# Trunk layer in fp32 on one core: the gate block z in a two-product form, and weights and read-outs ranked ahead of the scan

## The chip, the cores and the metric

The kernel runs on one core of a Trainium2 chip. The metric is the device time of one execution in microseconds (us). TensorE is called PE here, VectorE DVE, ScalarE ACT, GpSimd POOL and SyncE SP, as in the profile.

## The reference, cut to what matters

One trunk layer for 256 positions of width 2048: a bidirectional SSD mixer, a cross-attention into 256 memory tokens, a ConvGLU channel mixer, and a final norm. The change lies in the mixer's input part:

```python
proj = u @ w_in
z, xbc, dt_raw = jnp.split(proj, [SSD_INNER, SSD_INNER + SSD_CONV_DIM], axis=-1)
xbc = jax.nn.silu(dwconv(xbc, conv_w, conv_b))
xs, Bm, Cm = jnp.split(xbc, [SSD_INNER, SSD_INNER + SSD_GROUPS * SSD_STATE], axis=-1)
...
y = y_f + y_b + xs * d_skip[:, None]
y = rmsnorm(y.reshape(b, s, SSD_INNER) * jax.nn.silu(z), norm_g)
return y.astype(u.dtype) @ w_out
```

The 4096 columns of z and of xs fall into 8 groups of 512 columns; y_f and y_b are a chunked scan over two chunks of 128 positions in either direction.

## The kernel before, in words

**Products.** Every fp32 operand of the large matrix products is split into a high and a low part, both in fp32r, and a product is the sum of high x high, high x low and low x high. Weights come in raw chunks of 1024 elements a partition (512 KB): `load_weights` has SP fetch the chunk into `raw` (5 buffers), ACT cast it to `w_hi` (L106) and DVE subtract to get `w_lo` (L107); `w_hi` and `w_lo` have 4 buffers each. One chunk serves 8 pairs of a contraction tile of 128 rows and an output tile of 128 features.

There are two forms for a pair. `gemm_feat` takes three matmuls of 256 columns (L152 to L154), each with its own load of weights into PE, and leaves the sum in 256 columns of PSUM: 512 output features fill one `psg` tile (2 banks). `gemm_feat_wide` takes two: `w_hi` against the high and low halves of the activations side by side, 512 columns (L169), and `w_lo` against the high half, 256 columns (L171). The two 256-column halves of its result must then be added: `add_halves` copies one out of PSUM on ACT (L177) and adds the other on DVE (L178). Here 256 features fill a `psg` tile. `psg` has two buffers in all (`ps_g`).

**Groups.** The loop over 8 groups runs project(g+1), project_z(g), scan_group(g). `project` makes xs (512 columns) and bc (256 columns), both in the three-product form, and puts them through the convolution (L362 to L373). `project_z` makes the gate `sz`, one buffer: a multiplication by the norm's factor straight from PSUM on DVE (L386) and a SiLU on ACT (L387). `scan_group` transposes xs and B (L405, L413) and copies them out (L406, L407, L414), forms the chunk states (L419, L420) and then, for each of the two chunks: fetches `r`, a 1 MB broadcast of the decays (L424, one buffer, so its fetch waits for L444 of the chunk before), works on it on ACT and DVE (8 times L435 and L436, then the exponential L438), builds `t` (L441, L442, L444), and multiplies (L448, L453). The results are put together on DVE (L456, L459, L460), where L459 reads `er`, a second broadcast fetched by SP (L398, four transfers, one buffer, free after L460 of the scan before). At the end L464 multiplies by `sz`, and L211, L101 and L102 square and split the result into the activations of the next product. That is w_out, whose first half uses `gemm_feat`.

**What sets the order.** The program is written as above, and a scheduler spreads the instructions of each engine into one fixed order each, by their place in the program and a model of the time. Each engine runs its list in order, and waits where an instruction's operands or buffers are not ready. So a group's scan lies between the matmuls of the next group's projections.

Of the kernel before, what the change touches and what calls it, by code (L numbers as in the profile page):

```python
# [1 line left out]

# [7 lines left out]
F32R = mybir.dt.float32r  # L10
AF = mybir.ActivationFunctionType
ALU = mybir.AluOpType
AX = mybir.AxisListType

P = 128
T = 256
# [20 lines left out]
def kernel(  # L37
# [15 lines left out]
    nc = tc.nc  # L53
# [9 lines left out]
    def sb(pool, shape, tag, dtype=F32, **kw):  # L63
        return pool.tile(shape, dtype, tag=tag, name=tag, **kw)
# [40 lines left out]
    def split_plain(hi, lo, src):  # L105
        nc.scalar.copy(out=hi, in_=src)  # L106
        nc.vector.tensor_tensor(out=lo, in0=src, in1=hi.bitcast(F32), op=ALU.subtract)  # L107

    def load_raw(wv, k0, cols):
        width = sum(n for _, n in cols)  # L110
        kc = 1024 // width
        raw = sb(ring_raw, [P, kc, width], "raw")
        at = 0
        for c0, n in cols:
            nc.sync.dma_start(out=raw[:, :, at:at + n], in_=wv[:, k0:k0 + kc, c0:c0 + n])
            at += n
        return raw

    def load_weights(wv, k0, cols, raw=None):
        width = sum(n for _, n in cols)  # L120
        kc = 1024 // width
        if raw is None:
            raw = load_raw(wv, k0, cols)
        hi = sb(ring, [P, kc, width], "w_hi", F32R)
        lo = sb(ring, [P, kc, width], "w_lo", F32R)
        split_plain(hi, lo, raw)
        return hi, lo

    def kview(w):
# [2 lines left out]
    def gemm_feat(units, wv, cols, k_first=0, first_raw=None):  # L132

        width = sum(n for _, n in cols)
        nft = width // P
        kc = 1024 // width
        nk = 4 * len(units)
        ps = psum_g()
        banks = [ps[:, b, :] for b in range((nft + 1) // 2)]
        for k0 in range(0, nk, kc):  # L140
            hi, lo = load_weights(wv, k_first + k0, cols, first_raw if k0 == 0 else None)
            for kk in range(kc):
                kt = k0 + kk
                uh = units[kt // 4][0][:, kt % 4, :]
                ul = units[kt // 4][1][:, kt % 4, :]
                for ft in range(nft):
                    dst = banks[ft // 2][:, (ft % 2) * T:(ft % 2 + 1) * T]
                    wh = hi[:, kk, ft * P:(ft + 1) * P]
                    wl = lo[:, kk, ft * P:(ft + 1) * P]
                    first = kt == 0 and ft % 2 == 0  # L150
                    last = kt == nk - 1 and (ft % 2 == 1 or ft == nft - 1)
                    nc.tensor.matmul(dst, wh, uh, start=first, stop=False, skip_group_check=True)  # L152
                    nc.tensor.matmul(dst, wh, ul, start=False, stop=False, skip_group_check=True)  # L153
                    nc.tensor.matmul(dst, wl, uh, start=False, stop=last, skip_group_check=True)  # L154
        return banks
# [18 lines left out]

    def add_halves(dst, ps):

        nc.scalar.copy(out=dst, in_=ps[:, :, T:])  # L177
        nc.vector.tensor_tensor(out=dst, in0=ps[:, :, :T], in1=dst, op=ALU.add)  # L178

    def gemm_tok(units, wv, c0, k_first=0):  # L180

# [16 lines left out]
    def two(bank):  # L198
        return bank.rearrange("p (j t) -> p j t", t=T)

    def rows2(r):
        return r.unsqueeze(1).broadcast_to([P, 2, T])
# [24 lines left out]
    def inv_rms(pool, acc, dst, n, tags=("rs_v", "rs_s")):  # L227
        ps = psum_m()
        nc.tensor.matmul(ps[:, :T], ones, acc[:, 0, :], start=True, stop=False)
        nc.tensor.matmul(ps[:, :T], ones, acc[:, 1, :], start=False, stop=True)  # L230
        rsqrt_mean(pool, dst, ps[:, :T], n, tags)
# [9 lines left out]
    w_in_v = kview(w_in)  # L241
# [47 lines left out]
    with tc.tile_pool(name="ssd", bufs=1) as ssd:  # L289
# [85 lines left out]
        def project(g):  # L375
            xs = sb(ssd, [P, 4, T], "xs", bufs=2)
            conv_silu(gemm_feat(units_mix, w_in_v, [(INNER + g * 512, 512)]), [g * 4 + j for j in range(4)], xs)
            bc = sb(ssd, [P, 2, T], "bc", bufs=2)
            conv_silu(gemm_feat(units_mix, w_in_v, [(2 * INNER + g * P, P), (2 * INNER + 1024 + g * P, P)]),
                      [32 + g, 40 + g], bc)  # L380
            return xs, bc

        def project_z(g):
            sz = sb(ssd, [P, 4, T], "sz")
            for b, bank in enumerate(gemm_feat(units_mix, w_in_v, [(g * 512, 512)])):
                nc.vector.tensor_tensor(out=sz[:, 2 * b:2 * b + 2, :], in0=two(bank), in1=rows2(r_mix), op=ALU.mult)  # L386
                nc.scalar.activation(out=sz[:, 2 * b:2 * b + 2, :], in_=sz[:, 2 * b:2 * b + 2, :], func=AF.Silu)  # L387
            return sz

        ecum_v = ecum_d.rearrange("(d g j q) l -> g q d j l", d=2, g=GROUPS, q=2)  # L390
# [77 lines left out]
            units_y.append(unit)  # L468

        nxt = project(0)  # L470
        for g in range(GROUPS):
            cur = nxt
            if g + 1 < GROUPS:
                nxt = project(g + 1)
            sz = project_z(g)
            scan_group(g, *cur, sz)
        inv_rms(ssd, acc_y, r_ssd, INNER, ("cb", "b_tok"))


# [295 lines left out]
```

## Time and profile before

| | |
|---|---|
| median of 3 runs | 1865.58 us (1864.4 to 1865.98) |
| profiled execution | 1863.24 us, of which the span of the trace is 1861.5 us |
| PE busy, share of the span | 99% |
| DVE, ACT busy | 68%, 55% |
| DMA engines busy, mean | 62%, 193 GB/s |

Durations below come from the one profiled execution. A busy share is the part of the span in which an engine ran something; a matmul's duration in a row covers its way through the array, so matmuls that follow each other overlap, and the distance between two starts says what one costs.

### The profile page before, as it was taken

The page shows a single profiled execution, that of the slowest core. Times are in us where ns is not written, and L with a number is a line of the kernel's source. Part 1 is how long each engine was busy: PE and PEld are TensorE (multiplying, and loading weights), DVE is VectorE, ACT ScalarE, POOL GpSimd, SP SyncE. Part 2 cuts the span into 40 slices and gives each one's busy share as a digit, 9 for nine tenths or more (in the row PEclk, how much of TensorE's full clock was granted, in tenths as well). Part 3 has the DMA queues.
Part 4 walks back from the last instruction along what each step waited for, and adds up shares of the span by engine and source line. Part 5 has one row for each costly group of instructions (what it writes and reads, how often), then busy time and mean ns, then how long its engine had stood idle before and what let it go on. Part 6 is the DMA issues. An engine that isn't in the chain of part 4 may idle for free.

```text
span 1861.5 us, 29854 instructions
## 1 busy us (share of the span) xinstructions
PE 1842.3 (99%) x11821; PEld 1663.5 (89%) x11821; DVE 1264.2 (68%) x1792; ACT 1018.2 (55%) x1454; POOL 2.3 (0%) x11
## 2 busy tenths in 40 slices
PE   8999999999999999999999999999999999999997
PEld 8999999999999988888888888888888888888886
DVE  6878888988887756655555667666664456666654
ACT  6667667766775645444444455555553345555443
POOL 0000000000000000000000000000000000000000
PEclk9999999999999999999999999999999999999999
DMA  8667666766766765655655556566666666666563
GB/s 289 198 203 214 199 189 201 219 197 201 215 182 205 244 197 182 184 177 170 176 176 181 164 187 206 179 189 188 191 191 192 193 192 188 185 187 187 190 193 114
DMA packets 289708, 358.94 MB, mean 193 GB/s; under 512 B 11616, under 2 KB 210656, under 8 KB 289056
## 3 DMA queue, kind: packets, MB, share of 16 engines
q1 hardware_dynamic: 289488, 356.76, 62.3%
q8 instruction: 92, 1.51, 0.3%
q14 instruction: 48, 0.39, 0.1%
q0 software_dynamic: 80, 0.28, 0.1%
HBM read 352.60 MB, written 4.39 MB: 192 GB/s over the span
## 4 chain that ended last, share of the span: by engine, by line
PE 99%; DMA 0%; DVE 0%; ACT 0%; SPq 0%; issue 0%; DVEq 0%
PE psg L169 30%; PE psg L171 16%; PE psg L154 10%; PE psg L153 10%; PE psg L152 10%; PE psm L194 6%; PE psm L193 6%; PE psm L195 6%; PE psm L453 1%; PE psm L448 1%; PE psm L419 1%; PE psm L589 0%; PE psm L591 0%; PE psm L590 0%; DMA x<-in_x_dram 0%; PE psm L405 0%
## 5 line engine op out<-in xcount | busy, mean ns | idle before, releaser
L107 DVE TENSOR_TENSOR w_lo<-raw,w_hi 128x1024 fp32r<-128x1024 f32 x618 | 753.7, 1223 | 499.3 <-ACT w_hi L106 497.1
L106 ACT CAST w_hi<-raw 128x1024 fp32r<-128x1024 f32 x618 | 645.7, 1049 | 684.0 <-PE psg L169 314.5
L169 PE MATMUL psg<-unit,w_hi 128*128 128x512 f32 x2432 | 853.3, 396 | 0.0
L171 PE MATMUL psg<-unit,w_lo 128*128 128x256 f32 x2432 | 683.4, 281 | 0.0
L169 PEld LDWEIGHTS psg<-unit,w_hi 128*128 128x128 f32 x2432 | 456.3, 188 | 106.0
L171 PEld LDWEIGHTS psg<-unit,w_lo 128*128 128x128 f32 x2432 | 460.7, 189 | 0.2
L154 PE MATMUL psg<-unit,w_lo 128*128 128x256 f32 x1552 | 444.8, 287 | 0.1
L152 PE MATMUL psg<-unit,w_hi 128*128 128x256 f32 x1552 | 442.4, 285 | 0.0
L153 PE MATMUL psg<-unit,w_hi 128*128 128x256 f32 x1552 | 441.6, 285 | 0.0
L154 PEld LDWEIGHTS psg<-unit,w_lo 128*128 128x128 f32 x1552 | 298.6, 192 | 3.4 <-issue 3.1
L152 PEld LDWEIGHTS psg<-unit,w_hi 128*128 128x128 f32 x1552 | 298.7, 193 | 1.7 <-issue 1.7
L153 PEld LDWEIGHTS psg<-unit,w_hi 128*128 128x128 f32 x1552 | 298.7, 193 | 0.3 <-issue 0.2
L195 PE MATMUL psm<-w_hi,unit 128*128 128x512 f32 x480 | 187.0, 390 | 0.0
L194 PE MATMUL psm<-w_lo,unit 128*128 128x512 f32 x480 | 187.0, 390 | 0.0
L193 PE MATMUL psm<-w_hi,unit 128*128 128x512 f32 x480 | 186.9, 389 | 0.0
L193 PEld LDWEIGHTS psm<-w_hi,unit 128*128 128x128 f32 x480 | 90.1, 188 | 18.9
L195 PEld LDWEIGHTS psm<-w_hi,unit 128*128 128x128 f32 x480 | 90.1, 188 | 18.8
L194 PEld LDWEIGHTS psm<-w_lo,unit 128*128 128x128 f32 x480 | 90.1, 188 | 18.4
L435 ACT ACTIVATE r<-r,ncum_tok 128x128 f32<-128x128 f32 x128 | 39.4, 390 | 57.5 <-DMA r<-cum_d 57.5
L436 DVE SCALAR_TENSOR_TENSOR r<-r,ncum_tok 128x128 f32<-128x128 f32 x128 | 37.0, 347 | 16.7 <-ACT r L435 16.7
L441 ACT ACTIVATE t<-cb,dt_tok 128x128 f32<-128x128 f32 x128 | 39.1, 389 | 0.7 <-DVE cb L428 0.2
L442 DVE SCALAR_TENSOR_TENSOR t<-cb,dt_tok,t 128x128 f32<-128x128 f32 x128 | 36.5, 349 | 3.3 <-ACT t L441 3.3
(222 smaller groups left out, 1076.4 us busy)
## 6 DMA issues: line engine op xcount, KB each, us to landing
raw<-in_w_up_dram SPq DMA_DIRECT2D x176, 512.0 KB, 3.7
raw<-in_w_in_dram SPq DMA_DIRECT2D x130, 512.0 KB, 4.6
raw<-in_w_down_dram SPq DMA_DIRECT2D x88, 512.0 KB, 3.8
raw<-in_w_out_dram SPq DMA_DIRECT2D x64, 512.0 KB, 4.2
raw<-in_wkv_dram SPq DMA_DIRECT2D x64, 512.0 KB, 3.8
raw<-in_w_in_dram SPq DMA_DIRECT2D x64, 256.0 KB, 4.4
r<-cum_d SPq DMA_DIRECT2D x16, 1024.0 KB, 6.3
raw<-in_wq_dram SPq DMA_DIRECT2D x32, 512.0 KB, 3.5
```

Source lines behind the costliest of these rows:

```text
L106: nc.scalar.copy(out=hi, in_=src)
L107: nc.vector.tensor_tensor(out=lo, in0=src, in1=hi.bitcast(F32), op=ALU.subtract)
L152: nc.tensor.matmul(dst, wh, uh, start=first, stop=False, skip_group_check=True)
L153: nc.tensor.matmul(dst, wh, ul, start=False, stop=False, skip_group_check=True)
L154: nc.tensor.matmul(dst, wl, uh, start=False, stop=last, skip_group_check=True)
L169: nc.tensor.matmul(ps[:, ft, :], hi[:, kk, fs], unit[2][:, kt % 4].rearrange("p s t -> p (s t)"), start=(kt == 0), stop=False, skip_group_ ...
L171: nc.tensor.matmul(ps[:, ft, :T], lo[:, kk, fs], unit[0][:, kt % 4, :], start=False, stop=(kt == nk - 1), skip_group_check=True)
L193: nc.tensor.matmul(banks[tt], uh, hi[:, kk, :], start=(kt == 0), stop=False)
L194: nc.tensor.matmul(banks[tt], uh, lo[:, kk, :], start=False, stop=False)
L195: nc.tensor.matmul(banks[tt], ul, hi[:, kk, :], start=False, stop=(kt == nk - 1))
L435: nc.scalar.activation(out=t1[:, h, :], in_=t1[:, h, :], func=AF.Identity, bias=ncum_tok[:, c, hf:hf + 1])
L441: nc.scalar.activation(out=t2[:, h, :], in_=cb[:, 1, :], func=AF.Copy, scale=dt_tok[:, c, hb:hb + 1])
```

## The change

z is computed in the two-product form, in two halves of 256 columns, each read out by `add_halves`; L386's multiplication and the SiLU then work in SBUF. While the groups run, a chunk's fetch and split and the read-outs of `add_halves` are ranked as if they stood 500 instructions earlier in the program, so the scheduler puts them ahead of work of the scan with which they compete. Outside the groups nothing is ranked.

```diff
--- before.py
+++ after.py
@@ -1,4 +1,4 @@
-from contextlib import ExitStack
+from contextlib import ExitStack, nullcontext
 
 import concourse.bass as bass
 import concourse.tile as tile
@@ -116,14 +116,21 @@
             at += n
         return raw
 
+    ahead = [0]
+
+    def urgent():
+
+        return tc.high_priority(offset=ahead[0]) if ahead[0] else nullcontext()
+
     def load_weights(wv, k0, cols, raw=None):
         width = sum(n for _, n in cols)
         kc = 1024 // width
-        if raw is None:
-            raw = load_raw(wv, k0, cols)
-        hi = sb(ring, [P, kc, width], "w_hi", F32R)
-        lo = sb(ring, [P, kc, width], "w_lo", F32R)
-        split_plain(hi, lo, raw)
+        with urgent():
+            if raw is None:
+                raw = load_raw(wv, k0, cols)
+            hi = sb(ring, [P, kc, width], "w_hi", F32R)
+            lo = sb(ring, [P, kc, width], "w_lo", F32R)
+            split_plain(hi, lo, raw)
         return hi, lo
 
     def kview(w):
@@ -174,8 +181,9 @@
 
     def add_halves(dst, ps):
 
-        nc.scalar.copy(out=dst, in_=ps[:, :, T:])
-        nc.vector.tensor_tensor(out=dst, in0=ps[:, :, :T], in1=dst, op=ALU.add)
+        with urgent():
+            nc.scalar.copy(out=dst, in_=ps[:, :, T:])
+            nc.vector.tensor_tensor(out=dst, in0=ps[:, :, :T], in1=dst, op=ALU.add)
 
     def gemm_tok(units, wv, c0, k_first=0):
 
@@ -382,9 +390,11 @@
 
         def project_z(g):
             sz = sb(ssd, [P, 4, T], "sz")
-            for b, bank in enumerate(gemm_feat(units_mix, w_in_v, [(g * 512, 512)])):
-                nc.vector.tensor_tensor(out=sz[:, 2 * b:2 * b + 2, :], in0=two(bank), in1=rows2(r_mix), op=ALU.mult)
-                nc.scalar.activation(out=sz[:, 2 * b:2 * b + 2, :], in_=sz[:, 2 * b:2 * b + 2, :], func=AF.Silu)
+            for b in range(2):
+                sv = sz[:, 2 * b:2 * b + 2, :]
+                add_halves(sv, gemm_feat_wide(units_mix, w_in_v, [(g * 512 + b * 256, 256)]))
+                nc.vector.tensor_tensor(out=sv, in0=sv, in1=rows2(r_mix), op=ALU.mult)
+                nc.scalar.activation(out=sv, in_=sv, func=AF.Silu)
             return sz
 
         ecum_v = ecum_d.rearrange("(d g j q) l -> g q d j l", d=2, g=GROUPS, q=2)
@@ -468,12 +478,14 @@
             units_y.append(unit)
 
         nxt = project(0)
+        ahead[0] = 500
         for g in range(GROUPS):
             cur = nxt
             if g + 1 < GROUPS:
                 nxt = project(g + 1)
             sz = project_z(g)
             scan_group(g, *cur, sz)
+        ahead[0] = 0
         inv_rms(ssd, acc_y, r_ssd, INNER, ("cb", "b_tok"))
```

The lines of the gemm functions move by 7 (L152 becomes L159, L169 L176, L177 L185, L178 L186), those of the convolution by 8 and those of the scan by 10 (L435 becomes L445).

The rows that follow are each engine's list: the line, the operation, output and inputs, the output's shape, the engines or DMA queues whose semaphores it waits for (the number 49 is only the program's), and how many like it follow each other.

**PE, last group.** PE's list from the transposes of the last scan (L405) on, before; `psg` is there the first tile of w_out, `psm` tiles belong to the scan:

```order
L405 MATMUL psm<-ident,xs 128x128 [waits PE_49]
L405 MATMUL psm<-ident,xs 128x128 x3
L405 MATMUL psm<-ident,xs 128x128 [waits PE_49]
L405 MATMUL psm<-ident,xs 128x128 x3
L413 MATMUL psm<-ident,bc 128x128 [waits PE_49]
L413 MATMUL psm<-ident,bc 128x128
L154 MATMUL psg<-unit,w_lo 128x256
L152 MATMUL psg<-unit,w_hi 128x256
L153 MATMUL psg<-unit,w_hi 128x256
```

The same place with the change, where L415 is the transpose, L429 the states, L458 the multiplication with them, and L159 to L161 are w_out's first tile:

```order
L415 MATMUL psm<-ident,xs 128x128 [waits PE_49]
L415 MATMUL psm<-ident,xs 128x128 x3
L415 MATMUL psm<-ident,xs 128x128 [waits PE_49]
L415 MATMUL psm<-ident,xs 128x128 x3
L423 MATMUL psm<-ident,bc 128x128 [waits PE_49]
L423 MATMUL psm<-ident,bc 128x128
L429 MATMUL psm<-xsd,b_tok 128x512 [waits DVE_49,Activation_49]
L429 MATMUL psm<-xsd,b_tok 128x512 [waits DVE_49,PE_49]
L436 MATMUL psm<-bc 128x128
L458 MATMUL psm<-bc,st 128x128 [waits Activation_49]
L458 MATMUL psm<-bc,st 128x128 x3
L159 MATMUL psg<-unit,w_hi 128x256 [waits DVE_49]
```

Before, w_out's matmuls of an already opened tile follow the transposes, 29 of them ahead of the first L419, 38 in all ahead of the second; with the change the scan's matmuls stand in a row, and the first matmul of w_out comes behind them and waits for DVE, where the one that releases its buffer is L186 of z's first half.

**ACT, last group.** ACT's list from the work on `r` (L435) on, before; L420 is the states' copy, L438 the exponential, L211 and L101 belong to the end of the scan before the last:

```order
L435 ACTIVATE r<-r,ncum_tok 128x128 [waits DMAHW1_49,DVE_49]
L414 COPY b_tok<-psm 128x256 [waits PE_49]
L435 ACTIVATE r<-r,ncum_tok 128x128 x7
L106 CAST w_hi<-raw 128x1024 [waits DMAHW7_49,PE_49]
L211 ACTIVATE sq<-xs 128x512 [waits DVE_49]
L101 ACTIVATE unit<-xs,par 128x256 x2
L101 ACTIVATE unit<-xs,par 128x256 [waits DVE_49]
L101 ACTIVATE unit<-xs,par 128x256
L420 COPY st<-psm 128x512 [waits PE_49]
L438 ACTIVATE r<-r 128x1024 [waits DVE_49]
L420 COPY st<-psm 128x512 [waits PE_49]
```

And with the change, where L445, L430, L448, L219 and L101 are the same work and L185 reads z out of PSUM:

```order
L445 ACTIVATE r<-r,ncum_tok 128x128 [waits DMAHW1_49,DVE_49,Activation_49]
L445 ACTIVATE r<-r,ncum_tok 128x128 x2
L424 COPY b_tok<-psm 128x256 [waits PE_49]
L445 ACTIVATE r<-r,ncum_tok 128x128 x5
L430 COPY st<-psm 128x512 [waits PE_49] x2
L448 ACTIVATE r<-r 128x1024 [waits DVE_49]
L219 ACTIVATE sq<-xs 128x512 [waits DVE_49]
L101 ACTIVATE unit<-xs,par 128x256 x2
L185 COPY sz<-psg 128x512 [waits DVE_49]
L185 COPY sz<-psg 128x512
L101 ACTIVATE unit<-xs,par 128x256 x2
```

Both read-outs of the last z now stand behind the work on `r`, and the first of them waits for DVE: L474 of the scan before the last, which reads `sz`. L474 in its turn stands on DVE behind all eight L446, the DVE part of the work on `r`.

**DVE, a group in the middle.** DVE's list around the wait for `r` (L436), before; L362 reads xs out of PSUM, L464 multiplies by `sz`, L107 makes `w_lo`:

```order
L362 TENSOR_TENSOR cv_s<-psg,r_mix 128x512 [waits PE_49]
L362 TENSOR_TENSOR cv_s<-psg,r_mix 128x512
L107 TENSOR_TENSOR w_lo<-raw,w_hi 128x1024 [waits DMAHW7_49,DMAHW0_49,Activation_49]
L456 SCALAR_TENSOR_TENSOR xs<-xs,par,psm 128x128 [waits PE_49]
L456 SCALAR_TENSOR_TENSOR xs<-xs,par,psm 128x128 x3
L436 SCALAR_TENSOR_TENSOR r<-r,ncum_tok 128x128 [waits DMAHW3_49,Activation_49]
L436 SCALAR_TENSOR_TENSOR r<-r,ncum_tok 128x128 [waits Activation_49] x2
L460 TENSOR_TENSOR xs<-xs,er 128x4x128 [waits DVE_49]
L436 SCALAR_TENSOR_TENSOR r<-r,ncum_tok 128x128 [waits Activation_49] x5
L464 TENSOR_TENSOR xs<-xs,sz 128x512 [waits DVE_49]
L464 TENSOR_TENSOR xs<-xs,sz 128x512
L107 TENSOR_TENSOR w_lo<-raw,w_hi 128x1024 [waits DMAHW1_49,PE_49,Activation_49]
```

With the change (L370 is the read-out of xs, L446 the work on `r`, L474 the multiplication by `sz`):

```order
L466 SCALAR_TENSOR_TENSOR xs<-xs,par,psm 128x128 [waits PE_49]
L466 SCALAR_TENSOR_TENSOR xs<-xs,par,psm 128x128 x3
L446 SCALAR_TENSOR_TENSOR r<-r,ncum_tok 128x128 [waits DMAHW2_49,Activation_49]
L470 TENSOR_TENSOR xs<-xs,er 128x4x128 [waits DVE_49]
L446 SCALAR_TENSOR_TENSOR r<-r,ncum_tok 128x128 [waits Activation_49] x2
L370 TENSOR_TENSOR cv_s<-psg,r_mix 128x512 [waits PE_49]
L370 TENSOR_TENSOR cv_s<-psg,r_mix 128x512
L446 SCALAR_TENSOR_TENSOR r<-r,ncum_tok 128x128 [waits Activation_49]
L474 TENSOR_TENSOR xs<-xs,sz 128x512 [waits DVE_49]
L474 TENSOR_TENSOR xs<-xs,sz 128x512
L446 SCALAR_TENSOR_TENSOR r<-r,ncum_tok 128x128 [waits Activation_49] x4
L107 TENSOR_TENSOR w_lo<-raw,w_hi 128x1024 [waits DMAHW7_49,DMAHW0_49,Activation_49]
```

The read-out of xs has moved from ahead of the wait for `r` to behind it, and the `w_lo` that used to stand between the read-out and the wait now comes last. Ahead of this place ACT's list has one more cast of a chunk between the work on `r` and the exponential than before.

## Rows read from the trace of the kernel before

**Rows 1.** The page's busy times (part 1) and the chain that ended last (part 4).

```profile
PE 1842.3 (99%) x11821; PEld 1663.5 (89%) x11821; DVE 1264.2 (68%) x1792; ACT 1018.2 (55%) x1454; POOL 2.3 (0%) x11
...
PE 99%; DMA 0%; DVE 0%; ACT 0%; SPq 0%; issue 0%; DVEq 0%
```

**Rows 2.** Timeline of PE in a three-product stretch: start, duration, line, tiles.

```profile
150.05 0.28 PE L152 MATMUL psg<-unit,w_hi 128*128 128x256 f32 x1
...
150.41 0.28 PE L152 MATMUL psg<-unit,w_hi 128*128 128x256 f32 x1
```

**Rows 3.** Busy time of L169 by window, and its timeline at the ends.

```profile
1180.00:1340.00 160.00, 160.00 (x463) 1.00 0.63 190
...
1180.15 0.39 PE L169 MATMUL psg<-unit,w_hi 128*128 128x512 f32 x1
...
1339.96 0.39 PE L169 MATMUL psg<-unit,w_hi 128*128 128x512 f32 x1
```

**Rows 4.** The page's groups of instructions: busy us, mean ns of one.

```profile
L169 PE MATMUL psg<-unit,w_hi 128*128 128x512 f32 x2432 | 853.3, 396 | 0.0
```

**Rows 5.** Groups of instructions of ACT and DVE: busy us, mean ns of one.

```profile
L177 ACT COPY f_s<-psg 128x512 f32<-128x512 f32 x44 | 25.4, 578 | 0.2 <-DVE r_ffn L225 0.2
L438 ACT ACTIVATE r<-r 128x1024 f32<-128x1024 f32 x16 | 16.9, 1059 | 0.1
L101 ACT ACTIVATE unit<-xs,par 128x256 fp32r<-128x256 f32 x32 | 13.7, 497 | 0.0
L420 ACT COPY st<-psm 128x512 f32<-128x512 f32 x16 | 9.4, 585 | 16.2 <-PE psm L419 16.2
L211 ACT ACTIVATE sq<-xs 128x512 f32<-128x512 f32 x15 | 9.3, 623 | 1.6 <-DVE xs L464 1.6
...
L178 DVE TENSOR_TENSOR f_s<-psg,f_s 128x512 f32<-128x512 f32 x44 | 30.1, 683 | 0.0
```

**Rows 6.** One period of the groups by window: PE, PEld, DVE, ACT busy; clock.

```profile
440.92:505.95 65.03, 65.03 (x549) 63.47 (x547) 55.07 (x101) 44.87 (x79) 0.00 (x0) 1.00 0.67 203
```

**Rows 7.** Timelines of SP, PE, ACT and DVE around the wait for r, middle group.

```profile
339.22 0.37 SPq L424 DMA_DIRECT2D r<-cum_d  x1
...
341.01 1.09 PE L453 MATMUL psm<-t,xs_tok 128*64 128x128 f32 x16
...
352.93 0.28 PE L154 MATMUL psg<-unit,w_lo 128*128 128x256 f32 x1
...
346.20 2.46 ACT L435 ACTIVATE r<-r,ncum_tok 128x128 f32<-128x128 f32 x8 [5.07 <-DMA r<-cum_d]
...
341.38 1.28 DVE L362 TENSOR_TENSOR cv_s<-psg,r_mix 128x512 f32<-128x512 f32 x2
...
350.61 2.35 DVE L107 TENSOR_TENSOR w_lo<-raw,w_hi 128x1024 fp32r<-128x1024 f32 x2
```

**Rows 8.** Timelines of SP, PE and ACT at the last group.

```profile
533.94 0.37 SPq L424 DMA_DIRECT2D r<-cum_d  x1
...
539.74 2.66 SPq L398 DMA_DIRECT2D er<-ecum_d  x4
...
536.09 1.09 PE L453 MATMUL psm<-t,xs_tok 128*64 128x128 f32 x16
537.11 1.10 PE L405 MATMUL psm<-ident,xs 128*128 128x128 f32 x8
...
540.55 0.40 ACT L435 ACTIVATE r<-r,ncum_tok 128x128 f32<-128x128 f32 x1 [1.67 <-DMA r<-cum_d]
540.86 0.35 ACT L414 COPY b_tok<-psm 128x256 f32<-128x256 f32 x1
```

**Rows 9.** The tile er: time of its 32 transfers from issue to landing.

```profile
DMA to landing us min/median/max: 3.0/3.7/8.0
```

**Rows 10.** Timeline of PE at the last scan's second product.

```profile
577.04 1.09 PE L453 MATMUL psm<-t,xs_tok 128*64 128x128 f32 x16 [1.48 <-DVE t L444]
```

**Rows 11.** Window near the start: PE, PEld, DVE, ACT, POOL busy; granted clock.

```profile
6.00:10.00 4.00, 2.94 (x12) 1.73 (x10) 2.33 (x6) 3.38 (x11) 0.00 (x0) 1.00 1.08 344
```

## The prediction

> **What bounds the kernel now.** I read the page's busy times first, then the chain that ended last: PE is busy for 99% of the span and the chain is PE for 99% [rows 1]. So a microsecond taken from PE's stream is a microsecond of the kernel, and so is each that PE has to wait; DVE, ACT and DMA matter only where PE waits for them. Next I read the cost of a matmul, and not from its duration. The groups give 396 ns for the 512-column matmul [rows 4], but such durations overlap. Starts tell more: in a three-product stretch L152 comes again after 0.36 us [rows 2], three matmuls and so 0.120 each. In the two-product form 462 starts of L169 lie between 1180.15 and 1339.96 (463 touch the window, one of them begun before it), so 461 pairs take 159.81 us, 0.3467 each [rows 3]. Last I read the period of a group, 65.03 us, in which PE is busy throughout, DVE 55.07 and ACT 44.87 [rows 6]: no engine but PE is full, yet DVE is not far from it, and orders and buffers decide whether its work comes in time.
>
> **What z saves.** z has 8 x 64 = 512 pairs. Each falls from 0.3600 to 0.3467 us: 512 x 0.0133 = 6.8 us, 0.85 a group. Both forms stream 768 columns a pair, so the gain is only that of one weight load fewer. The Trainium skill speaks against even this: TensorE: Matmul & The Clock Gate, section Back-to-back issue gap, gives an isolated matmul N/2.4 + 2.5 ns, by which a pair would save 2.5 ns and z 1.3 us. The starts here, 120 ns where that formula has 109, differ from it, and the sum goes by the starts.
>
> **What z adds.** Two copies on ACT at 578 ns and two additions on DVE at 683 ns a group [rows 5]. DVE goes from 55.1 to 56.4 us of a period of some 64, ACT from 44.9 to 46.0. That is hidden behind PE as long as the order lets it, so I cost it at nothing by itself, and 1.4 us a group (11 in all) if all of it came onto PE's path. What it costs is in the waits. z needs two psum tiles instead of one, and only two exist. So the second half waits until bc has been read out, the next xs until the first half has been, and after the last group w_out's first tile until z's first half has been.
>
> **The middle groups.** There DVE's last weights before a long wait for r are the narrow place. Before, the second L453 of a scan starts at 341.01, the w_lo behind the wait is ready at about 351.8 (the two take 350.61 to 352.96) and PE takes it at 352.93: 1.1 us to spare [rows 7]. r's fetch is issued at 339.22 and ACT reads it at 346.20, so the wait is a transfer of 7.0 us. With the change PE comes to its w_lo 0.5 us later (one three-product more ahead of L463, and 20 + 72 + 2 behind it). But xs's two read-outs, 1.28 us, now follow the wait instead of filling it, and one more cast (about 0.95) stands ahead of the exponential, so r is free and fetched again that much later. 1.1 + 0.5 - 1.28 - 0.95 = -0.6: PE waits about 0.6 us, or nothing if the cast is absorbed. The second half of z waits for bc's read-out a little behind, by the same lateness. I take 0.55 for the four scans in this order (third to sixth): 2.2 us, bounds 0 and 4.
>
> **The second group** has an order of its own. The last cast of z's second half takes the buffer that the first half's last chunk gives free, and on ACT it stands ahead of z's read-out and of the B copy for L429, which here comes ahead of the second half. From the first half's end: cast 1.0, two copies 0.58 each, B copy 0.35 [rows 5, 8], so L429 at +2.5, while PE has 0.65 of transposes. PE waits 1.9 us, once, plus 0.4 as in the middle groups: 2.3, bounds 1 and 3.
>
> **The last group** is the largest term. Let X be the start of the scan-before-last's second L453, 536.09 before. PE then does this and the transposes, until X + 2.3. r, issued 2.15 ahead of X, is read at X + 4.46 [rows 8]. Before, PE filled this time with w_out. With the change w_out's first tile needs L186, which needs L185, which waits for sz to be read by L474, behind r. After r's arrival ACT has eight L445 (2.46), the B copy 0.35, two state copies 1.17, the exponential 1.06, a square 0.62, two splits 0.85 as spaced and the read-out 0.58 [rows 5, 7]: 7.1, so L185 ends at X + 11.5 and L186 at X + 12.2 at the earliest. Ahead of L186 DVE also has L469, which needs er. er can only be fetched after L470, at about X + 5.9; its four issues take 2.66 [rows 8] and the landing 3.0 to 8.0, median 3.7 [rows 9]. The third or fourth counts, issued 1.3 to 1.9 later, and two instructions of 0.4 and 0.68 follow L469's 0.68. That gives X + 13.3 at the median and X + 17 at the slow end. At the end of the wait for r the queues carry raw chunks too, so I take one more than the median: X + 14.3. Between X + 2.3 and then PE has only L429, L436 and L458, 3.2 us. PE idles 14.3 - 2.3 - 3.2 = 8.8 us (6.7 to 11.7). Behind it the chain r, exponential, t is late in turn: PE's 53 three-products (6.4) against about 7 on DVE, 0.6 us, and at the very last product about 2.0, where 1.48 is waited now [rows 10]: 0.5 net. The tail costs +9.9, bounds 7.5 and 13.
>
> **Sum.** -6.8 + 2.2 + 2.3 + 9.9 = +7.6 us. On the profiled execution's 1863.2 this gives 1870.8; the median of the runs is 2.3 above that execution, so on it 1865.6 + 7.6 = **1873.2**, 0.4% slower. A measurement of this kernel can tell about 0.2%, 3.7 us, from no change: under 1861.9 is faster, over 1869.3 slower.
>
> **The rivals.**
> *The tail alone.* The middle groups lose nothing, since the cast finds a gap on ACT and r is not later, and the tail lands at its low end: -6.8 + 1 + 7.5 = +1.7, 1867. ACT is busy for two thirds of a period only, which speaks for it; that DVE waited for the exponential in this place before speaks against. 20%.
> *Faster: r comes before PE needs it.* The whole stall hangs on r's fetch, issued 2.15 ahead of X. The last z is 1.4 us longer between the two L463 than the three-products that stood there, and if PE is late at X by 4.5 us more, r is there when the transposes are done: then er and ACT's list are early too, and the tail costs at most 3. -6.8 + 2.3 + 0.5 = -4, 1861.6, without middle stalls. The point is r's arrival at X + 2 or earlier. The steady distance of 15 us between the two products is the loop of r itself (fetch, work, exponential), so PE has no reason to be so late: 10%.
> *The clock.* Two idle stretches of 3.5 and about 5 us in a row are longer than any of PE's in the groups now. If the granted clock fell to its lower level, 1.2 GHz, about 3 us of matmuls would take twice as long: +3, 1876. Against it, near the start PE was busy for 2.94 us of 4 and the granted clock stayed at 1.00, 2.4 GHz [rows 11]; no row has a gap of 5 us. TensorE: Matmul & The Clock Gate of the Trainium skill, section Part 1: The HAM clock gate, says that an idle array falls back to the lower level; the trace neither shows nor excludes it here. 7%.
> *z gains nothing.* If the 512-column matmul cost twice a 256-column one here, 0.240, the pair would stay at 0.36 and the time would be 1865.6 + 14.4 = 1880. The rows of the other products have it at 0.23 [rows 3]. The Trainium skill's formula above would give nearly this case, 1879, by its 2.5 ns a pair. 3%.
> The forecast keeps 60%.
>
> **Range and chances.** 1866 to 1877.5 holds the forecast with its bounds (middle 0 to 4, tail 7.5 to 13 give 1868 to 1878, both ends unlikely together), the tail alone, and most of the clock case; what is left out is the faster rival and the ends. Slower by over 0.2%: the forecast but for its low end, the clock and the last rival, 66%. Within: 23%. Faster: 11%.
>
> **What would show it.** L176's starts in z 0.347 us apart; PE idle once for some 2 us in the second group and for about half a microsecond a period later on; and, behind the last scan-before-last product, PE waiting for ACT (b_tok), then for DVE (sz), with 6.7 to 11.7 us between the transposes and w_out's first matmul beside the scan's own. I am wrong if that stretch is short, if DVE, 88% full, falls behind so far that PE waits for w_lo in every group by more than 1 us, or if z's pairs stay at 0.36.

## The result, and the profile after

With the change the kernel takes 1880.66 us (median of 4 runs, 1877.68 to 1881.09); the kernel before, in 4 runs on the same chip, 1864.99 (1863.44 to 1865.98). The ratio is 1.0086, interval [1.0074, 1.0098]: 15.7 us slower. The forecast said slower, by 7.6; 1880.66 lies above its range. One run of `e4` below (2265.22 us) and one of `e22` (4703.56 us) were in a slow state and are left out of the times given for them. The profiled execution took 1880.57 us, 17.3 more than the one of before.

The page of the kernel after: the busy times and the head of the chain that ended last.

```profile
span 1878.9 us, 28863 instructions
...
PE 1844.1 (98%) x11309; PEld 1639.5 (87%) x11309; DVE 1274.9 (68%) x1808; ACT 1024.5 (55%) x1470; POOL 2.3 (0%) x11
...
PE 95%; DVE 2%; DMA 1%; ACT 1%; issue 0%; DVEq 0%; ACTq 0%; POOLq 0%
```

Against [rows 1] the chain has lost 4 of its 99 hundredths of PE to other engines. What PE waited for in the kernel after (total us, times, longest):

```profile
PE psm L429 <- ACT b_tok L424: 6.5, 2, 4.8
...
PE psg L176 <- DVE sz L186: 3.2, 1, 3.2
PE psg L159 <- DVE sz L186: 2.7, 1, 2.7
PE psm L463 <- DVE t L454: 1.8, 2, 1.5
PE psg L161 <- DVE w_lo L107: 1.3, 2, 1.0
```

These are few and long waits, not one in every group. Windows of the kernel after (length; busy PE, PEld, DVE, ACT, POOL; granted clock; DMA share; GB/s): a middle group, two pieces of the second group, then the tail in steps of 5 us.

```profile
331.88:396.46 64.58, 64.58 (x483) 60.07 (x482) 56.40 (x103) 45.45 (x80) 0.00 (x0) 1.00 0.69 205
...
173.00:177.50 4.50, 1.14 (x3) 0.34 (x3) 4.50 (x8) 2.68 (x5) 0.00 (x0) 0.71 0.75 223
177.50:181.50 4.00, 4.00 (x13) 3.42 (x14) 4.00 (x9) 2.03 (x4) 0.00 (x0) 0.50 0.46 140
...
545.00:550.00 5.00, 1.39 (x2) 0.84 (x3) 3.24 (x10) 2.68 (x9) 0.00 (x0) 0.69 0.88 331
550.00:555.00 5.00, 4.30 (x13) 2.30 (x11) 2.68 (x7) 3.19 (x7) 0.00 (x0) 0.62 0.41 120
555.00:560.00 5.00, 2.75 (x13) 2.75 (x14) 5.00 (x12) 4.98 (x15) 0.00 (x0) 0.72 0.00 0
```

The middle group is 0.45 us shorter than the 65.03 of [rows 6], with PE busy throughout and DVE at 56.40, the 56.4 forecast. The loss is elsewhere: where PE has idled, the granted clock is down to 0.50, which is 1.2 GHz.

**The second group.** Timeline of PE in the kernel after: the last transposes, the states, and the first pairs of z's second half.

```profile
171.04 0.38 PE L423 MATMUL psm<-ident,bc 128*128 128x128 f32 x2
173.14 1.12 PE L429 MATMUL psm<-xsd,b_tok 128*128 128x512 f32 x2 [1.72 <-ACT b_tok L424]
177.49 0.77 PE L176 MATMUL psg<-unit,w_hi 128*128 128x512 f32 x1 [3.22 <-DVE sz L186]
...
181.46 0.52 PE L176 MATMUL psg<-unit,w_hi 128*128 128x512 f32 x1
```

ACT's and DVE's timelines over the same time:

```profile
171.75 0.58 ACT L185 COPY sz<-psg 128x512 f32<-128x512 f32 x1
...
172.71 0.38 ACT L424 COPY b_tok<-psm 128x256 f32<-128x256 f32 x1
...
168.52 2.05 DVE L377 SCALAR_TENSOR_TENSOR xs<-cv_s,par,xs 128x254 f32<-128x254 f32 x5
170.49 1.22 DVE L107 TENSOR_TENSOR w_lo<-raw,w_hi 128x1024 fp32r<-128x1024 f32 x1
...
173.20 1.22 DVE L107 TENSOR_TENSOR w_lo<-raw,w_hi 128x1024 fp32r<-128x1024 f32 x1
174.34 1.26 DVE L379 SCALAR_TENSOR_TENSOR xs<-cv_s,par,xs 128x255 f32<-128x255 f32 x3
175.52 1.22 DVE L107 TENSOR_TENSOR w_lo<-raw,w_hi 128x1024 fp32r<-128x1024 f32 x1
176.66 0.68 DVE L186 TENSOR_TENSOR sz<-psg,sz 128x512 f32<-128x512 f32 x1
```

ACT's half of the read-out is done at 172.33, close to the forecast. DVE's half, L186, starts at 176.66, in the first place that its list has for it: DVE is busy from 157.16 on without a gap (19.50 of the 19.50 us up to 176.66), with splits of weights and the convolution. PE waits 3.22 us for it, and the next six pairs, 177.49 to 181.46, take 3.97 us where 6 x 0.3467 make 2.08.

**The last group.** Timelines of PE, ACT, DVE and SP in the kernel after. X, the start of the scan-before-last's second product, is 541.46 here.

```profile
543.42 0.38 PE L423 MATMUL psm<-ident,bc 128*128 128x128 f32 x2
548.61 3.78 PE L429 MATMUL psm<-xsd,b_tok 128*128 128x512 f32 x4 [4.81 <-ACT b_tok L424]
...
557.25 0.58 PE L159 MATMUL psg<-unit,w_hi 128*128 128x256 f32 x1 [2.71 <-DVE sz L186]
...
547.32 0.98 ACT L445 ACTIVATE r<-r,ncum_tok 128x128 f32<-128x128 f32 x3 [3.06 <-DMA r<-cum_d]
548.21 0.35 ACT L424 COPY b_tok<-psm 128x256 f32<-128x256 f32 x1
...
550.72 0.58 ACT L430 COPY st<-psm 128x512 f32<-128x512 f32 x1 [0.69 <-PE psm L429]
552.43 0.59 ACT L430 COPY st<-psm 128x512 f32<-128x512 f32 x1 [1.12 <-PE psm L429]
552.91 1.06 ACT L448 ACTIVATE r<-r 128x1024 f32<-128x1024 f32 x1
...
555.18 1.06 ACT L185 COPY sz<-psg 128x512 f32<-128x512 f32 x2
...
554.52 0.69 DVE L220 TENSOR_TENSOR acc_y<-acc_y,sq 128x512 f32<-128x512 f32 x1 [1.24 <-ACT sq L219]
555.13 0.48 DVE L102 SCALAR_TENSOR_TENSOR unit<-xs,par,unit 128x256 fp32r<-128x256 f32 x1
555.52 0.68 DVE L469 TENSOR_TENSOR er<-psm,er 128x512 f32<-128x512 f32 x1
...
556.52 1.28 DVE L186 TENSOR_TENSOR sz<-psg,sz 128x512 f32<-128x512 f32 x2
...
538.87 0.37 SPq L434 DMA_DIRECT2D r<-cum_d  x1
...
549.02 2.57 SPq L408 DMA_DIRECT2D er<-ecum_d  x4
```

The four transfers of `er` issued here, from issue to landing:

```profile
DMA to landing us min/median/max: 3.5/3.6/3.9
```

This is the stall that the prediction described, about 1.5 us later: r is read at X + 5.86 and w_out's first matmul starts at X + 15.8. The link that came last is another one. The last `er` transfer, issued at 551.0, landed by 554.9, and L469 ran at 555.52 in its turn. DVE had no gap from L220 at 554.52 to L186, and L220 waited for ACT's square. ACT was late because r was, and because its two copies of the states waited 0.69 and 1.12 us for PE's L429. Before, PE went from [rows 8]'s transposes straight into w_out.

**Where the time went.** I cut PE's time at the scans' products (L463, before L453) and set each stretch against what its matmuls would cost at the distances of undisturbed stretches (0.120, 0.3467 a pair, the scan's matmuls as spaced where nothing waits). What is over, the excess, is waits and clock. The row on z is such a count, no measurement: it uses the forecast's own distances. Change of this excess, before to after, in us:

| stretch (us in the trace after) | forecast | measured |
|---|---|---|
| work saved in z, by count | -6.8 | -6.8 (1459.97 to 1453.16) |
| second group: 134.75 to 202.76 | +2.3 | +9.2 (scan 0's second product 1.6, z and the scan behind it 7.6) |
| third group: 202.76 to 267.26 | in the next | +2.1 |
| the other middle groups | +2.2 with the third | +1.1 |
| last group: from 541.46 | +9.9 | +10.4 (12.34 and 0.16, less the 2.05 of before) |
| sum | +7.6 | +16.0 |

The remaining 1.3 of 17.3 us lie ahead of the first and behind the last product.

### The profile page after: what moved, and what is told of

It reads as the page before. It is cut to its first block, busy times and chain, and to the rows that moved or that the text cites. A ratio compares the mean times of both kernels' runs of the same rounds, so it can differ in the third digit from the quotient of the medians.

```text
span 1878.9 us, 28863 instructions
## 1 busy us (share of the span) xinstructions
PE 1844.1 (98%) x11309; PEld 1639.5 (87%) x11309; DVE 1274.9 (68%) x1808; ACT 1024.5 (55%) x1470; POOL 2.3 (0%) x11
## 3 DMA queue, kind: packets, MB, share of 16 engines
q8 instruction: 88, 1.44, 0.3%
## 4 chain that ended last, share of the span: by engine, by line
PE 95%; DVE 2%; DMA 1%; ACT 1%; issue 0%; DVEq 0%; ACTq 0%; POOLq 0%
PE psg L176 36%; PE psg L178 18%; PE psg L161 6%; PE psg L160 6%; PE psg L159 6%; PE psm L203 6%; PE psm L201 6%; PE psm L202 6%; DMA r<-cum_d 1%; PE psm L429 1%; PE psm L458 1%; PE psm L463 1%; DVE w_lo L107 0%; PE psm L603 0%; PE psm L601 0%; PE psm L602 0%
## 5 line engine op out<-in xcount | busy, mean ns | idle before, releaser
L107 DVE TENSOR_TENSOR w_lo<-raw,w_hi 128x1024 fp32r<-128x1024 f32 x618 | 754.1, 1224 | 507.1 <-ACT w_hi L106 502.9
L176 PE MATMUL psg<-unit,w_hi 128*128 128x512 f32 x2944 | 1035.5, 396 | 3.4 <-DVE sz L186 3.2
L178 PE MATMUL psg<-unit,w_lo 128*128 128x256 f32 x2944 | 828.1, 281 | 0.0
L176 PEld LDWEIGHTS psg<-unit,w_hi 128*128 128x128 f32 x2944 | 553.6, 188 | 131.8 <-issue 4.0
L178 PEld LDWEIGHTS psg<-unit,w_lo 128*128 128x128 f32 x2944 | 558.2, 190 | 0.5
L159 PE MATMUL psg<-unit,w_hi 128*128 128x256 f32 x1040 | 296.5, 286 | 2.7 <-DVE sz L186 2.7
L161 PE MATMUL psg<-unit,w_lo 128*128 128x256 f32 x1040 | 297.2, 286 | 1.3 <-DVE w_lo L107 1.3
L160 PE MATMUL psg<-unit,w_hi 128*128 128x256 f32 x1040 | 296.9, 286 | 0.0
L159 PEld LDWEIGHTS psg<-unit,w_hi 128*128 128x128 f32 x1040 | 200.5, 193 | 3.2 <-DVE sz L186 2.9
L161 PEld LDWEIGHTS psg<-unit,w_lo 128*128 128x128 f32 x1040 | 200.5, 193 | 2.3 <-DVE w_lo L107 1.9
L160 PEld LDWEIGHTS psg<-unit,w_hi 128*128 128x128 f32 x1040 | 200.5, 193 | 1.2 <-issue 1.1
L445 ACT ACTIVATE r<-r,ncum_tok 128x128 f32<-128x128 f32 x128 | 39.5, 389 | 71.7 <-DMA r<-cum_d 67.2
L446 DVE SCALAR_TENSOR_TENSOR r<-r,ncum_tok 128x128 f32<-128x128 f32 x128 | 38.2, 349 | 24.7 <-ACT r L445 24.6
L451 ACT ACTIVATE t<-cb,dt_tok 128x128 f32<-128x128 f32 x128 | 39.2, 390 | 4.5 <-DVE cb L438 4.5
```

Source lines behind the costliest of these rows:

```text
L176: nc.tensor.matmul(ps[:, ft, :], hi[:, kk, fs], unit[2][:, kt % 4].rearrange("p s t -> p (s t)"), start=(kt == 0), stop=False, skip_group_ ...
L178: nc.tensor.matmul(ps[:, ft, :T], lo[:, kk, fs], unit[0][:, kt % 4, :], start=False, stop=(kt == nk - 1), skip_group_check=True)
L445: nc.scalar.activation(out=t1[:, h, :], in_=t1[:, h, :], func=AF.Identity, bias=ncum_tok[:, c, hf:hf + 1])
L451: nc.scalar.activation(out=t2[:, h, :], in_=cb[:, 1, :], func=AF.Copy, scale=dt_tok[:, c, hb:hb + 1])
```

## The experiments

The theory after the result: the tail's loss comes from the one `sz` buffer, the second group's from DVE's backlog in front of L186, each enlarged by the clock, and the ranking adds nothing to either. The rivals: the ranking makes the loss; two `psg` tiles instead of one make it; the loss belongs to the second group's place and goes away with its form. Each run was timed beside the kernel before on its own chip (1862.57 for `e1`, `e2`, `e3` and `e5`, 1863.06 for `e4`, `e6`, `e14` and `e15`, 1863.4 for `e22` and `e23`, 1863.16 for `e17` and `e17u`).

**Each part alone.** `e1_z_alone`: the two-product z without the ranking.

```diff
-        ahead[0] = 500
+        ahead[0] = 0
```

> z in the two-product form as in the change, nothing ranked. Theory: the loss comes from PE waiting for PSUM read-outs, in the second group (about 9 us, 2 of it at the lower granted clock) and in the last (about 10.5 us more than before); these follow from z's form and from the buffers, and PE's list is the same as with the change up to the last group: 1878 to 1883 us, with both stretches in the trace. Rival: the ranking pushes the scan's work back and so makes the waits: then this is at or under 1866 us.

Measured: 1879.41 us, 1.0089 [1.0073, 1.0106]. The excess is 7.45 in the second group's long stretch and 12.79 in the tail, where the whole change has 7.6 and 12.34. The form of z makes the loss by itself.

`e2_rank_alone`: the ranking with z in three products.

```diff
             sz = sb(ssd, [P, 4, T], "sz")
+            if g in (0, 1, 2, 3, 4, 5, 6, 7):
+                for b, bank in enumerate(gemm_feat(units_mix, w_in_v, [(g * 512, 512)])):
+                    ...
+                return sz
```

> z in the three-product form as before, weights ranked as in the change (nothing in the groups uses the ranked read-outs then). Theory: no read-out that PE has to wait for is added, 1863 to 1869 us. Rival (the ranking does the harm): 1872 us or more, with PE waiting for w_lo or t in every group.

Measured: 1878.28 us, 1.0082 [1.0067, 1.0097]. My expectation missed and the rival's came: the ranking alone loses about as much as z alone, and the two losses do not add. What PE waited for in this run (its lines stand 5 below those of the kernel after: L468 is the product, L450 the first reader of r):

```profile
PE psm L468 <- DVE t L459: 7.7, 8, 1.5
...
PE psm L434 <- ACT b_tok L429: 2.3, 1, 2.3
```

ACT's timeline of it, where r arrives in one group:

```profile
207.22 2.45 ACT L450 ACTIVATE r<-r,ncum_tok 128x128 f32<-128x128 f32 x8 [6.58 <-DMA r<-cum_d]
```

Here every scan waits for t, which hangs on r. The r read at 207.22 was issued at 197.30, 9.9 us earlier; its transfer has a median of 7.8 us in this run, 6.3 before and 6.5 with the whole change.

`e23_rank_alone_half_r`: the same with half of r fetched. It leaves out one direction's decays.

```diff
-                nc.sync.dma_start(out=r, in_=cum_v[c, g].partition_broadcast(P))
+                nc.sync.dma_start(out=r[:, 0], in_=cum_v[c, g, 0].partition_broadcast(P))
...
-                    nc.vector.scalar_tensor_tensor(out=t1[:, h, :], in0=r[:, 1, h, :], scalar=ncum_tok[:, c, hb:hb + 1],
+                    nc.vector.scalar_tensor_tensor(out=t1[:, h, :], in0=tri[:, 1, :], scalar=-1.0,
```

> The ranking alone, with only one of r's two halves fetched (0.5 MB instead of 1 MB; the other operand is replaced by a constant tile, so the scan's decays are left out in one direction, the instructions and their number stay). Theory: ranked alone, PE waits for t at each scan's second product, since r lands late (median 7.8 us instead of 6.3, up to 9.8) beside the raw chunks that were ranked ahead of it; with half the bytes these waits go, and most of the 15.7 us: 1863 to 1868. Rival (the ranking makes DVE's and ACT's order bad, whatever r does): 1873 or more.

Measured: 1861.88 us, 0.9991 [0.9982, 1.0], a little under what I expected. PE waits for nothing but the start; r lands in 5.3 us at the median. So the ranking's own loss is in the main r coming late. The run changes more than that: the order between the products moved a little (93 matmuls for 98), and DVE's L451 takes 0.29 us instead of 0.35, so the size is not r's alone. Why r is in time again when the two parts are together is not settled.

**The tail.** `e3_last_z_old`: the whole change, but the last group's z in three products (the block above with `if g in (7,)`).

> The change, with the last group's z in the three-product form. Theory: the last group's wait goes (10.5 us back, 0.85 us of saving lost), the second group's stays: 1871 us (1869 to 1873). Rival (every two-product z costs the same share, through the load on DVE and ACT): one eighth of the 16 us comes back, 1878.7 us.

Measured: 1870.14 us, 1.0042 [1.0027, 1.0057]; the tail's excess is 1.59 instead of 12.34. `e5_last_gate_elsewhere` keeps the two-product form there and writes its halves to two other buffers.

```diff
+            halves = [sz[:, 2 * b:2 * b + 2, :] for b in range(2)]
+            if g == GROUPS - 1:
+                halves = [sb(ssd, [P, 2, T], "cv_s", bufs=2) for _ in range(2)]
             for b in range(2):
-                sv = sz[:, 2 * b:2 * b + 2, :]
+                sv = halves[b]
...
```

> The change, with the last group's gate written to the two buffers of the convolution's input, which are free by then, instead of the single sz; its form stays two-product, and it still takes both PSUM tiles. Theory: the read-out no longer waits for the scan before to read sz behind r, w_out's first matmuls fill the time again: 1870 us (1868 to 1873). Rival (two PSUM tiles at once are the cause, not sz): 1876 us or more, with PE still waiting for L186 in the last group.

Measured: 1869.33 us, 1.0037 [1.0024, 1.005]; excess 1.54. Its windows over the time in which the kernel after idles:

```profile
545.00:550.00 5.00, 5.00 (x44) 5.00 (x43) 5.00 (x13) 4.98 (x12) 0.00 (x0) 1.00 0.88 292
550.00:555.00 5.00, 5.00 (x35) 4.04 (x33) 4.58 (x7) 4.99 (x9) 0.00 (x0) 1.00 0.64 163
```

PE is busy and the clock at 1.00: w_out's matmuls are back in this time. This run still needs two `psg` tiles for z, so their number is not the cause; the wait of L185 for `sz` is.

`e22_filler_tail`: 16 matmuls of 512 columns ahead of the last scan's states, their result unused, to keep PE from idling.

```diff
+            if g == GROUPS - 1:
+                warm_ps = psum_m()
+                for i in range(WARM):
+                    nc.tensor.matmul(warm_ps, units_mix[0][0][:, 0, :P], ...)
```

> The change, with 16 more matmuls of 512 columns (0.23 us each, 3.7 us in all, their result is not used) that stand on PE between the last scan's transposes and its first L429, in time in which PE waits for the B copy anyway; L186 is as late as before, behind r. Theory: the low granted clock after the idle stretch is a cost of its own: with the fillers the clock stays at its upper level there and 2 to 3 us of the last group's loss go: 1876 to 1878.5 on a chip where before is at 1862.6 to 1863 and the change at 1878 to 1880. Rival: the clock costs nothing by itself, since everything there waits for r, ACT and DVE: no difference, or a loss by what the fillers exceed the wait.

Measured: 1876.87 us (1873.95 to 1878.73), 1.0078 [1.0065, 1.0091]. Windows of this run:

```profile
545.00:550.00 5.00, 3.99 (x16) 2.49 (x14) 4.56 (x12) 4.43 (x12) 0.00 (x0) 1.00 0.66 225
550.00:555.00 5.00, 3.80 (x32) 3.80 (x33) 5.00 (x12) 5.00 (x14) 0.00 (x0) 1.00 0.08 24
```

The clock stays at 1.00, and the tail's excess is 7.47, with 3.7 of fillers in it. The run does not price the clock all the same. Its interval overlaps that of the whole change, and two other things moved: r is read 4.10 us after the scan-before-last's second product instead of 5.86, and the instruction that reads `er` (L475 there, L469 with the change) stands behind z's read-out instead of ahead of it, so w_out starts after 11.5 us instead of 15.8.

**The second group.** `e4_second_z_old`: z in three products in the second group alone (`if g in (1,)`).

> The change, with z of the second group alone in the three-product form. In the program's lists the scheduler then gives the third group the order that the second had (the first L429 ahead of z's second half, the read-outs of z and bc on DVE behind most of the convolution). Theory: the loss of the second group belongs to that order, a read-out queued on DVE behind a backlog, so it moves to the third group and the time stays: 1877 to 1882 us on a chip where before has 1862.6 to 1865. Rival (the second group loses because the stretch near the start is short of data): 8 us come back, about 1871.

Measured: 1882.33 us, 1.0101 [1.0083, 1.012], at the upper end of what I expected. The second group is clean (excess 0.08), and the third now has 8.24. Its PE and DVE there:

```profile
243.90 0.76 PE L176 MATMUL psg<-unit,w_hi 128*128 128x512 f32 x1 [3.77 <-DVE sz L186]
...
241.94 1.22 DVE L107 TENSOR_TENSOR w_lo<-raw,w_hi 128x1024 fp32r<-128x1024 f32 x1
243.07 0.68 DVE L186 TENSOR_TENSOR sz<-psg,sz 128x512 f32<-128x512 f32 x1
```

The loss moved with its mechanism, L186 behind L107 and the convolution. `e6_three_z_old` takes the old form in the first, second and last groups (`if g in (0, 1, 7)`).

> The change, with z of the first two groups and of the last in the three-product form. Theory: the last group's loss goes as in the run with only the last one old, the third group has the order that loses, so 5 to 9 us above before: 1868 to 1872. Rival (loss in the second group is the start's): within 2 us of before or under it.

Measured: 1875.63 us, 1.0069 [1.0055, 1.0083], above what I expected: the third group's excess is 9.39, and the tail keeps about 3.4, with a wait of 2.1 us for xsd in it. So neither of the two runs loses the stall by sparing the second group; it goes to the next group with a split z.

`e14_act_readout` takes DVE out of the read-out: ACT copies both halves and DVE adds in SBUF; the last z has the old form.

```diff
...
-                add_halves(sv, gemm_feat_wide(units_mix, w_in_v, [(g * 512 + b * 256, 256)]))
+                ps = gemm_feat_wide(units_mix, w_in_v, [(g * 512 + b * 256, 256)])
+                half = sb(ssd, [P, 2, T], "sq")
+                with urgent():
+                    nc.scalar.copy(out=sv, in_=ps[:, :, T:])
+                    nc.scalar.copy(out=half, in_=ps[:, :, :T])
+                    nc.vector.tensor_tensor(out=sv, in0=half, in1=sv, op=ALU.add)
```

> The last z in the three-product form, and in the other seven both PSUM halves copied out by ACT (one copy of 0.58 us more each), so that DVE adds them from SBUF and PSUM is free without DVE. Theory: the second group's wait for DVE's backlog goes, about 7 of the 7.6 us that the kernel with the last z old is above before; what is left is about the saving of 6 us less some single microseconds of waits at the scans: within 3 us of before. Rival (PE is held by something else there, the weights or r): 6 us or more above before, as with DVE's read-out.

Measured: 1870.3 us, 1.0041 [1.0028, 1.0053]. The expectation missed, and the time is the rival's. The second group's excess falls from 6.77 (`e3`) to 2.25, but other waits give it back: t 2.7 us, w_lo 2.4, a unit of ACT 2.2, ACT's own read-out 1.5. `e15_act_readout_unranked` is the same with `ahead[0] = 0`.

> As the run with ACT's read-outs, nothing ranked. Theory: with the two-product z the ranking makes no difference (z alone was as slow as the change): within 2 us of the ranked one. Rival: the ranking costs by itself (ranked alone, 15.7 us): 5 us or more under the ranked one.

Measured: 1873.41 us (1868.18 to 1875.6), 1.005 [1.0036, 1.0064]. That is 3.1 us above the ranked run where I expected 2 at most, but the intervals overlap: no difference is shown. `e17_one_act_readout` reads out by ACT twice in the second group alone, and leaves `add_halves` elsewhere; `e17u_one_act_readout_unranked` is that with `ahead[0] = 0`.

```diff
...
+                ps = gemm_feat_wide(units_mix, w_in_v, [(g * 512 + b * 256, 256)])
+                if g in (1,):
+                    half = sb(ssd, [P, 2, T], "sq")
+                    nc.scalar.copy(out=sv, in_=ps[:, :, T:])
+                    nc.scalar.copy(out=half, in_=ps[:, :, :T])
+                    nc.vector.tensor_tensor(out=sv, in0=half, in1=sv, op=ALU.add)
+                else:
+                    add_halves(sv, ps)
```

> The change with the last z in the three-product form, and in the second group alone both PSUM halves copied out by ACT, as in the run with ACT's read-outs. PE's list then has the usual order in the second group and that of the change in the middle ones. Theory: the second group's 7 us go without the middle groups' waits that ACT's extra copies brought: 1 to 3 us above before, or level with it (1862 to 1866 where before has 1863). Rival (ACT's copies were not what helped there): 1868 to 1871 as with the last z old alone.

> The same with nothing ranked. Theory (the two-product z with or without ranking has nearly the same lists): within 2 us of the ranked one. Rival: 3 us or more under it.

Measured: 1865.98 us, 1.0013 [1.0004, 1.0022], and 1865.15, 1.0009 [1.0, 1.0018], both as expected. The interval of `e17` lies below that of `e3`, whose program differs from it by the second group's read-out alone. From `e17`, PE's timeline at the place of the long wait, and where the states (L441 there) stand now:

```profile
171.70 0.50 PE L176 MATMUL psg<-unit,w_hi 128*128 128x512 f32 x1 [1.44 <-ACT sq L404]
...
183.12 1.88 PE L441 MATMUL psm<-xsd,b_tok 128*128 128x512 f32 x4
```

A window of `e17` over one middle group:

```profile
403.90:468.17 64.27, 64.27 (x484) 59.94 (x483) 56.15 (x104) 45.52 (x81) 0.00 (x0) 1.00 0.71 205
```

PE waits 1.44 us instead of 3.22. The states have moved behind z's second half, so the wait of 1.72 us for b_tok is gone as well: the scheduler's order changed with the read-out (in `e14` too), and no run separates the two. The tail still has 4.19 us of excess, of which PE waits 2.33 for xsd. No version that does all the work beat the kernel before.

## Why the prediction was right in sign and too small

**Right: what z saves.** The 6.81 us of the table are counted and confirm nothing; two measurements do. In the kernel after, the 64 pairs of z between 411.26 and 460.73 take 22.23 us, 0.347 each. And the group of `e17` in which PE waits for nothing is 0.76 us shorter than [rows 6], of the 0.85 forecast. By the formula of the Trainium skill that the prediction weighed (TensorE: Matmul & The Clock Gate, Back-to-back issue gap) a group would save 0.16, an estimate; the measurement decides for the starts.

**Right in size, by errors that cancel: the tail.** That the last read-out waits for `sz` behind r is as forecast, and `e5` shows it: without that wait the loss is gone. The terms inside were off. Up to w_out's start the excess was 10.7 us where 8.8 idle were forecast. The forecast had `er` arrive last; it did not, but r was read 1.4 us later than I took, and ACT's copies of the states waited 1.8 us for L429, which I had at nothing. PE itself waited 4.81 + 0.25 + 2.71 = 7.8 us; most of the rest of the 10.7 is matmuls at half clock (four L429 in 3.57 us from start to the next start, where the same four take 1.72 in a middle group of this kernel, 385.40 to 387.12). Behind w_out's start I had 0.6 for a wait, and 1.6 came: its 53 matmuls up to the next product took 8.0 us instead of 6.4, the first of them at half clock. Against both, the last product, for which I added 0.5, had no wait any more and gave back 1.9. Net 10.4 for 9.9: the sum is luck.

**Near in sum, by one group: the middle groups.** 3.2 us for 2.2, two thirds of it in the third group, where PE waits 1.0 us for w_lo at the forecast place. In the fourth to sixth, where 0.55 each was forecast, the trace has no such wait, and 0.03 to 0.4 us of excess.

**Wrong: the step "The second group".** It said "PE waits 1.9 us, once", from ACT's instructions alone. ACT was ready as computed. But a read-out by `add_halves` ends on DVE, and I never counted what stands ahead of L186 in DVE's list. DVE was forecast at 88% of a group, and in this place its list had no gap: L186 started 4.3 us after ACT's half was done. The trace shows the wait, `e4` and `e6` move it together with that order, and in `e17`, without DVE in that read-out, the excess falls from 6.77 to 2.01; the part of that fall that belongs to the changed place of the states is not known. Among its signs of being wrong the prediction did name a DVE that falls behind, but at w_lo and in every group. The term was 2.3 and measured 9.2: 4.9 us of waits (1.72 and 3.22), 1.9 in the pairs at half clock, 1.6 more at scan 0's second product, where t came 1.48 us late (r was read 9.0 us after its issue), and under 1 in the rest. The term was 6.9 short, of the 8.1 us by which the forecast was.

**The clock rival, given 7%, came true.** I had judged it by one window in which PE was busy for 2.94 of 4 us [rows 11], and the sum has the clock at nothing. In the second group the granted clock was 0.71 and then 0.50 after two waits (1.72 and 3.22 us) with 1.1 us of matmuls between them, at a cost of 1.9 us. The Trainium skill (TensorE: Matmul & The Clock Gate, Part 1: The HAM clock gate) says that an idle array falls back to the lower level; the trace agrees. In the tail I estimate 3.4 us, from the 1.8 that ACT's copies waited and the 1.6 of w_out, where the rival had 3; no run shows that price by itself. `e22` shows a clock of 1.00 where PE is kept busy.

**The ranking.** The forecast gave it no term of its own. Together with z it has none (`e1` and the change are alike), alone it costs 15.7 us, in the main by r's transfers (`e2`, `e23`). That cost is hidden here, and I have not shown by what.

## What to carry to other kernels

Price a read-out by the whole in-order list ahead of its last instruction, on each engine that takes part, and not by when its input is ready: DVE, 88% busy over a group here, had 19.5 us without a gap just there. A saving that is spread thin (0.85 us in each of 8 groups) is lost to one buffer with a single copy behind a transfer, so look at the first and the last turn of a loop, whose order differs from the steady one. Where a forecast has PE idle for several microseconds, price the matmuls that follow at the lower clock as well, and what waits for them on other engines.

## What the runs showed of the hardware that was not expected

The granted clock fell after less idling than I had thought. Windows of `e2_rank_alone` around one scan's second product, where PE waited 0.56 us for w_lo and then 1.48 for t:

```profile
213.50:216.72 3.22, 1.18 (x8) 0.80 (x7) 2.07 (x3) 3.21 (x4) 0.00 (x0) 0.95 0.41 106
216.72:219.65 2.93, 2.93 (x21) 2.60 (x21) 2.93 (x4) 1.43 (x2) 0.00 (x0) 0.50 0.68 272
219.65:223.00 3.35, 3.35 (x29) 3.35 (x29) 2.56 (x6) 0.18 (x1) 0.00 (x0) 0.98 0.81 287
```

PE was busy for 1.18 of 3.22 us, and the next 2.93 us ran at 0.50. A single wait of 1.48 us, as in [rows 10], left the clock at 1.00 in the kernel after too:

```profile
150.20:153.00 2.80, 2.79 (x30) 2.63 (x31) 2.80 (x4) 1.43 (x2) 0.00 (x0) 1.00 0.86 281
```

One transfer of r (1 MB) took 5.8 to 8.3 us from issue to landing before (median 6.3) and 5.7 to 9.8 (median 7.8) with the ranking alone; half of it took 3.5 to 6.1.
